# Expert stage of a transformer block: gathers in halves behind the products, both experts take rows back, other weight pages held for the accumulators

## The chip, the cores and the metric

One core of a Trainium2 chip runs the kernel. Its engines are TensorE (PE in the profile), VectorE (DVE), ScalarE (ACT), GpSimd (POOL) and SyncE (SP), which here issues nearly all DMA transfers. The metric is the device time of one execution in microseconds (us); lower is better.

## The reference

One block over 512 latent tokens of width 1024 (with 256 context tokens): modulation, two attentions in parallel, a layer norm, then a mixture of 16 experts in which each expert picks its 64 tokens, and a second layer norm. The change lies in the mixture:

```python
def ec_moe(h, w_router, b_router, w1, w3, w2):
    b, n, _ = h.shape
    cap = EC_CAPACITY * n // N_EXPERTS              # 64
    aff = jax.nn.softmax((h @ w_router + b_router).astype(jnp.float32), axis=-1)
    g, idx = lax.top_k(jnp.swapaxes(aff, 1, 2), cap)
    bidx = jnp.arange(b)[:, None, None]
    xe = h[bidx, idx]
    hid = jax.nn.silu(jnp.einsum('becd,edf->becf', xe, w1)) * jnp.einsum('becd,edf->becf', xe, w3)
    ye = jnp.einsum('becf,efd->becd', hid, w2) * g[..., None].astype(h.dtype)
    return jnp.zeros_like(h).at[bidx, idx].add(ye)

x = layer_norm(ALPHA * x + g1 * o_lat, ln1_g, ln1_b)
x = layer_norm(ALPHA * x + g2 * ec_moe(x * (1.0 + sc2) + sh2, *moe), ln2_g, ln2_b)
```

All is float32. w1, w3 and w2 are 1024 x 1024 for each expert, 201 MB in all.

## The kernel before, in words

The expert stage is the last part of the kernel, from about 557 us on. It works through eight pairs of experts. A weight matrix comes in 8 pieces of 128 x 1024 (512 KB each), by `load` (line 940), so a pair takes 48 pieces: 32 of w1 and w3 (the up products), 16 of w2 (the down products).

**Pages.** `order` is the list of the pieces in the order of their use. Pieces go into a ring of 36 SBUF pages (`prefetch`); a page is used again when TensorE has read the piece in it. SyncE issues the loads one after the other, so a load whose page is still in use holds back all behind it. Nine more pieces are loaded ahead, once, into the places of tiles that are needed only later (`hold`, `places`): the four accumulators `acc0` to `acc3`, the tiles `gb`, `ye`, `hid`, `ohT` and `hidT`. The key in `places` is the position in `order`: 0 to 15 are w1 and w3 of expert 0 in turn, 16 to 31 those of expert 1, 32 to 39 w2 of expert 0, 40 to 47 w2 of expert 1. A held piece gives its place to the tile when it has been read, but frees no page of the ring. So 45 pieces are loaded before the first product ends.

**One pair.** `gather` makes a one-hot matrix `oh` on VectorE (L1133) and lets TensorE pick the pair's 128 token rows, transposed, out of `xn` (L1143): eight steps ("eighths") of 4 matmuls; after four and after eight of them VectorE writes `xe` (L1148). `up_` multiplies with w1 and w3 (L1180): eight steps k of two pieces; ScalarE and VectorE make `hid` (L1182, L1183). `back` scales `oh` on GpSimd (L1155) and transposes it (L1160) for putting rows back. `hid_t` transposes `hid` (L1188). `down` multiplies with w2 (L1196). `scatter` scales and splits the result on VectorE and ScalarE and gives four steps of two matmuls (L1209), each added to an accumulator on VectorE (L1210), for one half of the columns. The rows of a pair are put back during the next pair (`waiting`).

**Order.** TensorE's order is that of the code; the other engines' is a scheduler's. `base`, called once after the first pair's up products, loads ln1's scale and shift by GpSimd's queue and writes the first value of the accumulators: GpSimd the left half of the columns, VectorE the right (L1222, L1223). It ends with `spread` (L118), two matmuls that broadcast g2 into `g2b`.

Of the kernel before, what the change touches and what calls it, by code (L numbers as in the profile page):

```python
# [10 lines left out]
F32 = mybir.dt.float32  # L11
# [13 lines left out]
KD = D // 128  # L25
# [27 lines left out]
def _layer(tc, A, out, opened):  # L53
# [62 lines left out]
    def spread(dst, i, p, ps):  # L116

        T.matmul(ps, one2[p:p + 1, 0:1].to_broadcast([1, 128]), rm[i][p:p + 1, :], start=True, stop=True)  # L118
        S.activation(dst, ps, AF.Copy)
# [691 lines left out]
    for h in range(HEADS):  # L811
        pr = h // 2
# [86 lines left out]
    for c in range(4):  # L899
        hl = wos[c]  # L900
        for jj in range(2):
# [3 lines left out]
            g = yt.tile([128, 512], F32, name="gy")  # L905
# [19 lines left out]
    order[-2 * KD:] = [(E_N - 2 + i, "w2", (q, kh)) for q, p in enumerate(PARTS) for kh in range(KD // p[2]) for i in range(2)]  # L925
    loaded = {}

    places = {2: "gb", 5: "ye", 8: "acc0", 10: "acc1", 12: "acc2", 13: "hid", 16: "acc3", 21: "ohT", 27: "hidT"}
    order_r = [i for i in range(len(order)) if i not in places]
    N_RING = N_PG + N_WS + N_PG2 + N_PG3  # L930
    ring = [0]
# [1 line left out]
    def load(i, t):  # L933
        e, nm, k = order[i]
        if isinstance(k, tuple):
            q, kh = k
            c0, w, ks = PARTS[q]
            dma(t[:, :ks * w].rearrange("p (k n) -> p k n", k=ks), wsrc[nm][e, :, ks * kh:ks * kh + ks, c0:c0 + w])
        else:
            dma(t, wsrc[nm][e, :, k, :])  # L940
        loaded[e, nm, k] = t

    def place(nm):
        return rM if nm in ("gb", "acc0") else rM2 if nm[:3] == "acc" else me

    def hold(nm):
        load(next(i for i in places if places[i] == nm), place(nm).tile([128, D], F32, name="wr", tag=nm, bufs=1))
# [166 lines left out]
    psd, _ = pool("psd", space=PSUM)  # L1114
# [3 lines left out]
        return rM2.tile(shape or [128, D], dt, name=name, tag="pg3", bufs=N_PG3)  # L1118


    for nm in ("acc1", "acc2", "acc3"):
        hold(nm)
    prefetch(N_PG3)
    for nm in ("ye", "hid", "ohT", "hidT"):
        hold(nm)
    acc = [place(f"acc{t}").tile([128, D], F32, name="acc", tag=f"acc{t}", bufs=1) for t in range(NT)]

    def gather(pr):
# [23 lines left out]
    def back(pr, o):  # L1152

        e0 = 2 * pr
        G.tensor_tensor(o, o, aff[:, :, e0:e0 + 2, None].to_broadcast([128, NT, 2, CAP]), op=OP.mult)  # L1155
        ohT = me.tile([128, 2, SEQ], F32R, name="ohT")
        gt = me.tile([128, 2], F32, name="gate", bufs=2)
        ps = psd.tile([128, 512], F32, name="mx", bufs=3)
        for t in range(NT):
            T.transpose(ps[:, t * 128:(t + 1) * 128], o[:, t].rearrange("p e s -> p (e s)"), ident)  # L1160
        S.activation(ps, ps, AF.Copy, accum_out=gt[:, 0:1])
        V.tensor_scalar(ohT[:, 0, :], ps, 0.0, None, op0=OP.is_gt)
        if pr + 1 < E_N // 2:
            for e in range(2):
                a, b = slice(64 * e, 64 * e + 64), slice(64 - 64 * e, 128 - 64 * e)
                S.activation(ohT[b, 1, :], f(ohT[a, 0, :]), AF.Copy)
                S.activation(gt[b, 1:2], gt[a, 0:1], AF.Copy)
        return ohT, gt

    def up_(e, xe, hid, between=None, at=KD // 2):  # L1170

        sl = slice((e % 2) * CAP, (e % 2) * CAP + CAP)
        ph = [psd.tile([128, 512], F32, name="h", bufs=3) for _ in range(2)]
        for k in range(KD):
            if k == at and between:
                between()
            for i, n in enumerate(("w1", "w3")):
                w = piece(e, n, k)
                for hf in range(2):
                    T.matmul(ph[i][64 * hf:64 * hf + 64, :], xe[:, k, sl], w[:, hf * 512:(hf + 1) * 512],  # L1180
                             start=k == 0, stop=k == KD - 1)
        S.activation(hid[:, e % 2, :], ph[0], AF.Silu)  # L1182
        V.tensor_tensor(hid[:, e % 2, :], hid[:, e % 2, :], ph[1], op=OP.mult)  # L1183
# [15 lines left out]
    def scatter(py, ohT, gt, hf):  # L1199

        hs = slice(hf * 512, (hf + 1) * 512)
        ye = me.tile([128, 2, 512], F32R, name="ye")
        V.scalar_tensor_tensor(py[hf], py[hf], gt[:, hf:hf + 1], g2b[:, hs], op0=OP.mult, op1=OP.mult)  # L1203
        split(ye[:, 0, :], ye[:, 1, :], py[hf])

        def tile_(t):
            ps = psd.tile([128, 512], F32, name="mx", bufs=3)
            for i in range(2):
                T.matmul(ps, ohT[:, hf, t * 128:(t + 1) * 128], ye[:, i, :], start=i == 0, stop=i == 1)  # L1209
            V.tensor_tensor(acc[t][:, hs], acc[t][:, hs], ps, op=OP.add)  # L1210
        return [lambda t=t: tile_(t) for t in range(NT)]

    def base():

        gb = [me.tile([128, 2, 512], F32, name="gb0", tag="ye", bufs=1), rM.tile([128, 2, 512], F32, name="gb1", tag="gb", bufs=1)]
        for hf in range(2):
            for i, nm in enumerate(("ln1_g", "ln1_b")):
                G.dma_start(gb[hf][:, i], A[nm][:, hf * 512:(hf + 1) * 512].to_broadcast([128, 512]))
        for hf, eng in enumerate((G, V)):
            hs = slice(hf * 512, (hf + 1) * 512)  # L1220
            for t in range(NT):
                eng.tensor_tensor(acc[t][:, hs], xn[t][:, hs], gb[hf][:, 0], op=OP.mult)  # L1222
                eng.tensor_tensor(acc[t][:, hs], acc[t][:, hs], gb[hf][:, 1], op=OP.add)  # L1223
        g2b = rM.tile([128, D], F32, name="g2b", tag="gb", bufs=1)
        for g in range(2):
            spread(g2b[:, g * 512:(g + 1) * 512], 1, 64 + 32 * g, psd.tile([128, 512], F32, name="mx", bufs=3))
        return g2b

    def run(steps):
        for fn in steps:  # L1230
            fn()
# [3 lines left out]
    xe, o, steps = gather(0)  # L1235
    run(steps[:4])
    waiting = None
    for pr in range(E_N // 2):
        last = pr == E_N // 2 - 1
        hid = me.tile([128, 2, 512], F32, name="hid")  # L1240
        if waiting:
            s0 = scatter(*waiting, 0)
            up_(2 * pr, xe, hid, lambda: run(s0))
            run(scatter(*waiting, 1))
            ohT, gt = back(pr, o)
        else:
            up_(2 * pr, xe, hid, lambda: run(steps[4:]), 2)
        up_(2 * pr + 1, xe, hid)
        if not waiting:
            ohT, gt = back(pr, o)  # L1250
        hT = me.tile([128, 2, 4, 2, CAP], F32, name="hidT")
        hid_t(hid, hT, 0)
        if last:
            hid_t(hid, hT, 1)
            break
        xe, o, steps = gather(pr + 1)
        run(steps)
        hid_t(hid, hT, 1)
        if pr == 0:
            g2b = base()  # L1260
        py = [psd.tile([128, 512], F32, name="y", bufs=2) for _ in range(2)]
        for i in range(2):
            down(2 * pr + i, hT, py)
        waiting = py, ohT, gt
# [11 lines left out]
    ye = me.tile([128, 2, 512], F32R, name="ye")  # L1276
# [59 lines left out]
    for t in range(NT):  # L1336
        o = acc[t]
# [53 lines left out]
```

## Time and profile before

| what | value |
|---|---|
| median of 3 runs | 1047.92 us (1045.59 to 1049.13) |
| the profiled execution | 1046.86 us |
| its span, first to last instruction | 1045.0 us |
| PE, DVE, ACT, POOL busy | 94%, 43%, 26%, 17% of the span |
| loads of expert weights | 388, mostly 512 KB |

The profile is of one execution. The span is 1.86 us shorter than the execution's time. A busy PE is not a PE at its peak, and PE's instructions include ones that stretch while they wait for data. In the profile every matmul of the program in float32 is two instructions (the order below counts the program's).

### The profile page before, as it was taken

The numbers are of one execution on the slowest core, as the hardware profiler recorded it, in microseconds if no ns is written. First come the engines' busy times: TensorE is split into PE (matmuls) and PEld (weight loads), VectorE is DVE, ScalarE is ACT, GpSimd is POOL, SyncE is SP. The second block draws the span as 40 slices with busy tenths as digits, with TensorE's granted clock in tenths as the row PEclk, the third lists the DMA queues.
The fourth block names the chain that finished last, engine by engine and source line by source line (L and its number), as shares of the span: only waits on it lengthen the run. The fifth ranks groups of instructions, "written<-read, shape, count | busy, mean of one in ns | idle before, by whom it ended". The sixth has DMA issues, their size and how long they took to land.

```text
span 1045.0 us, 13829 instructions
## 1 busy us (share of the span) xinstructions
PE 981.9 (94%) x5280; PEld 618.1 (59%) x5280; DVE 445.7 (43%) x871; ACT 276.9 (26%) x556; POOL 173.7 (17%) x176
## 2 busy tenths in 40 slices
PE   6999998989899999999997999999999999999982
PEld 5888976868787777777754443535353534234331
DVE  2382366762677556558473413122213131111236
ACT  1222324224777555544110101010101010010010
POOL 2340020202576422210021400000000000000004
PEclk9999998999999999999998999999999999999996
DMA  9944337762012000038947989999999999999992
GB/s 298 291 155 131 98 113 250 233 200 82 21 31 66 22 20 22 21 107 305 393 177 308 377 307 409 409 409 409 408 409 409 410 409 409 409 410 409 408 367 100
DMA packets 101210, 266.98 MB, mean 255 GB/s; under 512 B 14020, under 2 KB 37528, under 8 KB 101144
## 3 DMA queue, kind: packets, MB, share of 16 engines
q1 hardware_dynamic: 100248, 264.52, 68.2%
q0 software_dynamic: 320, 1.05, 0.3%
q8 instruction: 42, 0.69, 0.3%
q10 hardware_dynamic: 576, 0.52, 0.1%
q14 instruction: 24, 0.20, 0.1%
HBM read 261.47 MB, written 2.10 MB: 252 GB/s over the span
## 4 chain that ended last, share of the span: by engine, by line
PE 71%; DMA 10%; issue 9%; DVE 5%; POOL 2%; ACT 2%; SPq 0%; POOLq 0%; DVEq 0%; ACTq 0%
PE h L1180 15%; PE y L1196 8%; DMA wr<-moe_w 6%; PE mx L1143 6%; PE acc L84 5%; PE acc L83 5%; PE acc L82 5%; PE sc L653 5%; DMA wa<-w_ada 3%; PE tpb L661 3%; PE av L843 2%; PE mx L1209 2%; PE av L778 2%; PE tp L237 1%; PE po L84 1%
## 5 line engine op out<-in xcount | busy, mean ns | idle before, releaser
L1180 PE MATMUL h<-wr,xe 128*64 128x512 f32 x1024 | 233.7, 598 | 8.6 <-DMA wr<-moe_w 7.5
L1180 PEld LDWEIGHTS h<-wr,xe 128*64 128x64 f32 x1024 | 68.3, 136 | 162.8 <-issue 105.7
L1196 PE MATMUL y<-wr,hidT 128*64 128x512 f32 x448 | 97.7, 594 | 0.0
L1183 DVE TENSOR_TENSOR hid<-hid,h 128x512 f32<-128x512 f32 x16 | 11.0, 686 | 146.8 <-PE h L1180 146.8
L642 DVE TENSOR_REDUCE nm<-sc 128x1 f32<-128x768 f32 x64 | 60.2, 954 | 30.7 <-PE sc L653 29.5
L1196 PEld LDWEIGHTS y<-wr,hidT 128*64 128x64 f32 x448 | 31.5, 137 | 61.8 <-issue 57.6
L1155 POOL TENSOR_TENSOR oh<-oh,aff 128x512 f32<-128x512 f32 x8 | 8.4, 1047 | 351.0 <-PE mx L1143 351.0
L643 ACT ACTIVATE P<-sc,nm 128x768 f32<-128x768 f32 x64 | 57.5, 900 | 29.0 <-DVE nm L642 21.8
L1143 PE MATMUL mx<-oh,xn 128*128 128x128 f32 x512 | 61.1, 282 | 1.4 <-DVE oh L1133 1.4
L1143 PEld LDWEIGHTS mx<-oh,xn 128*128 128x128 f32 x512 | 60.1, 198 | 2.5 <-issue 1.3
L75 ACT ACTIVATE whi<-wraw 128x1024 fp32r<-128x1024 f32 (+1 forms) x32 | 33.5, 1047 | 97.7 <-DMA wraw<-w_in 63.3
L78 DVE TENSOR_TENSOR wlo<-wraw,whi 128x1024 fp32r<-128x1024 f32 (+1 forms) x32 | 39.0, 1219 | 45.2 <-PE acc L83 29.4
L75 ACT ACTIVATE ye<-y 128x512 fp32r<-128x512 f32 (+2 forms) x17 | 9.7, 572 | 180.2 <-DVE y L1203 98.7
L1210 DVE TENSOR_TENSOR acc<-acc,mx 128x512 f32<-128x512 f32 x56 | 34.6, 680 | 42.0 <-PE mx L1209 42.0
L82 PE MATMUL acc<-xlh,whi 128*128 128x512 f32 x128 | 50.9, 398 | 1.6 <-ACT whi L75 1.6
L1182 ACT ACTIVATE hid<-h 128x512 f32<-128x512 f32 x16 | 9.6, 597 | 154.9 <-PE h L1180 154.9
L82 PE MATMUL acc<-whi,xlh 128*128 128x512 f32 (+1 forms) x128 | 49.6, 391 | 1.0 <-ACT whi L75 1.0
L84 PE MATMUL acc<-xlh,wlo 128*128 128x512 f32 x128 | 49.5, 394 | 0.8 <-DVE wlo L78 0.8
L83 PE MATMUL acc<-xll,whi 128*128 128x512 f32 x128 | 50.1, 391 | 0.0
L1203 DVE SCALAR_TENSOR_TENSOR y<-y,gate,g2b 128x512 f32<-128x512 f32 x14 | 9.9, 754 | 92.6 <-PE y L1196 92.6
L84 PE MATMUL acc<-whi,xll 128*128 128x512 f32 (+1 forms) x128 | 48.7, 381 | 0.5 <-POOL xll L78 0.5
L83 PE MATMUL acc<-wlo,xlh 128*128 128x512 f32 (+1 forms) x128 | 48.8, 381 | 0.2 <-DVE wlo L78 0.2
(341 smaller groups left out, 1699.3 us busy)
## 6 DMA issues: line engine op xcount, KB each, us to landing
wr<-moe_w SPq DMA_DIRECT2D x372, 512.0 KB, 10.2
wa<-w_ada SPq DMA_DIRECT2D x32, 512.0 KB, 4.4
wraw<-w_in SPq DMA_DIRECT2D x28, 512.0 KB, 5.1
wa<-w_ada SPq DMA_DIRECT2D x8, 1024.0 KB, 9.7
wr<-moe_w SPq DMA_DIRECT2D x16, 384.0 KB, 8.4
outraw<-w_out SPq DMA_DIRECT2D x8, 512.0 KB, 9.8
xq<-x SPq DMA_DIRECT2D x4, 512.0 KB, 7.9
q<-q SPq DMA_DIRECT2D x16, 128.0 KB, 2.2
```

The source lines that it names most:

```text
L75: S.activation(hi, src, AF.Copy)
L78: (eng_lo or V).tensor_tensor(lo, src, f(hi), op=OP.subtract)
L82: T.matmul(ps, lh, rh, start=start, stop=False)
L83: T.matmul(ps, lh, rl, start=False, stop=False)
L84: T.matmul(ps, ll, rh, start=False, stop=stop)
L642: V.tensor_reduce(nm, ps[:, :768], axis=AX.X, op=OP.max, negate=True)
L643: S.activation(p, ps[:, :768], AF.Exp, bias=nm, accum_out=z)
L653: T.matmul(ps[:, a:b], l, r[:, a:b], start=i == 0, stop=i == len(passes) - 1)
L1143: T.matmul(pss[hf][:, kk * 128:(kk + 1) * 128], xn[t][:, k * 128:(k + 1) * 128], o[:, t].rearrange("p e s -> p (e s)"), start=t == 0, stop ...
L1180: T.matmul(ph[i][64 * hf:64 * hf + 64, :], xe[:, k, sl], w[:, hf * 512:(hf + 1) * 512], start=k == 0, stop=k == KD - 1)
L1196: T.matmul(py[hf][r0:r0 + 64, :], hT[:, e % 2, fc % 4, fc // 4, :], w[:, hf * 512:(hf + 1) * 512], start=fc == 0, stop=fc == KD - 1)
L1210: V.tensor_tensor(acc[t][:, hs], acc[t][:, hs], ps, op=OP.add)
```

## The change

Three things change in the expert stage.

1. `places`: the four accumulators now hold w2 pieces (32 to 35) in place of early up pieces; `hid`, `ohT` and `hidT` hold up pieces 14, 29 and 30. All held pieces but two are loaded ahead of the last three pages of the ring.
2. From the second pair on, only the first four eighths of a gather stand between up and down products; the last four run inside the next pair's first expert, ahead of k = 3. The rows of the pair before are put back at k = 6 of the first expert (it was k = 4) and at k = 3 of the second expert (it was between the experts). `back` comes after both experts in every pair.
3. `base` no longer runs `spread`; its two matmuls run inside the second pair, behind the four eighths ahead of k = 3. Its loads come in the other order.

```diff
-    places = {2: "gb", 5: "ye", 8: "acc0", 10: "acc1", 12: "acc2", 13: "hid", 16: "acc3", 21: "ohT", 27: "hidT"}
+    places = {2: "gb", 5: "ye", 14: "hid", 29: "ohT", 30: "hidT", 32: "acc0", 33: "acc1", 34: "acc2", 35: "acc3"}
...
-    for nm in ("acc1", "acc2", "acc3"):
+    for nm in ("ye", "hid", "ohT", "hidT", "acc1", "acc2", "acc3"):
         hold(nm)
     prefetch(N_PG3)
-    for nm in ("ye", "hid", "ohT", "hidT"):
-        hold(nm)
...
-    def up_(e, xe, hid, between=None, at=KD // 2):
+    def up_(e, xe, hid, between={}):
...
         for k in range(KD):
-            if k == at and between:
-                between()
+            if k in between:
+                run(between[k])
...
-        for hf in range(2):
+        for hf in (1, 0):
             for i, nm in enumerate(("ln1_g", "ln1_b")):
...
         g2b = rM.tile([128, D], F32, name="g2b", tag="gb", bufs=1)
-        for g in range(2):
-            spread(g2b[:, g * 512:(g + 1) * 512], 1, 64 + 32 * g, psd.tile([128, 512], F32, name="mx", bufs=3))
-        return g2b
+        return g2b, [lambda g=g: spread(g2b[:, g * 512:(g + 1) * 512], 1, 64 + 32 * g, psd.tile([128, 512], F32, name="mx", bufs=3))
+                     for g in range(2)]
...
         if waiting:
-            s0 = scatter(*waiting, 0)
-            up_(2 * pr, xe, hid, lambda: run(s0))
-            run(scatter(*waiting, 1))
-            ohT, gt = back(pr, o)
+            rows_ = []
+            up_(2 * pr, xe, hid, {3: steps[4:] + spread_, 4: [lambda: rows_.extend(scatter(*waiting, 0))],
+                                  6: [lambda: run(rows_)]})
+            spread_ = []
+            rows_ = scatter(*waiting, 1)
+            up_(2 * pr + 1, xe, hid, {3: rows_})
         else:
-            up_(2 * pr, xe, hid, lambda: run(steps[4:]), 2)
-        up_(2 * pr + 1, xe, hid)
-        if not waiting:
-            ohT, gt = back(pr, o)
+            up_(2 * pr, xe, hid, {2: steps[4:]})
+            up_(2 * pr + 1, xe, hid)
+        ohT, gt = back(pr, o)
...
         xe, o, steps = gather(pr + 1)
-        run(steps)
+        run(steps[:4])
         hid_t(hid, hT, 1)
         if pr == 0:
-            g2b = base()
+            g2b, spread_ = base()
```

On TensorE, from the end of the first pair's up products (L1180 x56) to the middle of the second pair, the program before has these rows; the rows left out repeat the gather's matmul (L1143), 32 in all between the transposes.

```order
L1180 MATMUL h<-wr,xe 64x512 x56
L1160 MATMUL mx<-ident,oh 128x128 x4
L1188 MATMUL mx<-ident,hid 128x128 x4
L1143 MATMUL mx<-oh,xn_4497 128x128
...
L1188 MATMUL mx<-ident,hid 128x128 x4
L118 MATMUL mx<-rm,one_65 128x512 x2
L1196 MATMUL y<-wr,hidT 64x512 x32
L1180 MATMUL h<-wr,xe 64x512 x16
L1209 MATMUL mx<-ye,ohT 128x512 x8
```

The same place in the changed program, where L1141 is the gather (16 rows at each of its two places here), L1178 the up product, L1194 the down product and L1207 the rows put back.

```order
L1178 MATMUL h<-wr,xe 64x512 x56
L1158 MATMUL mx<-ident,oh 128x128 x4
L1186 MATMUL mx<-ident,hid 128x128 x4
L1141 MATMUL mx<-oh,xn_4497 128x128
...
L1186 MATMUL mx<-ident,hid 128x128 x4
L1194 MATMUL y<-wr,hidT 64x512 x32
L1178 MATMUL h<-wr,xe 64x512 x12
L1141 MATMUL mx<-oh,xn_4497 128x128
...
L118 MATMUL mx<-rm,one_65 128x512 x2
L1178 MATMUL h<-wr,xe 64x512 x12
L1207 MATMUL mx<-ye,ohT 128x512 x8
```

Sixteen gather matmuls and the two of `spread` have moved from ahead of the down products to behind the first three steps of the next up products, and the rows put back come at the seventh step, not the fifth.

On SyncE, these are the loads into the accumulators' places (the first three), the last pages and the other held tiles of the program before, with the first two loads into used pages behind them (the number is that of the tile, the right name the weight matrix).

```order
L940 DMA wr_5142<-moe_w1 128x1024
L940 DMA wr_5144<-moe_w1 128x1024
L940 DMA wr_5146<-moe_w1 128x1024
L940 DMA wr_5148<-moe_w2 128x1024
L940 DMA wr_5150<-moe_w2 128x1024
L940 DMA wr_5152<-moe_w2 128x1024
L940 DMA wr_5154<-moe_w3 128x1024
L940 DMA wr_5156<-moe_w3 128x1024
L940 DMA wr_5158<-moe_w3 128x1024
L940 DMA wr_5160<-moe_w3 128x1024
L940 DMA wr_5417<-moe_w2 128x1024
L940 DMA wr_5421<-moe_w2 128x1024
```

The same place in the changed program.

```order
L940 DMA wr_5150<-moe_w2 128x1024
L940 DMA wr_5152<-moe_w2 128x1024
L940 DMA wr_5154<-moe_w2 128x1024
L940 DMA wr_5156<-moe_w2 128x1024
L940 DMA wr_5142<-moe_w3 128x1024
L940 DMA wr_5144<-moe_w1 128x1024
L940 DMA wr_5146<-moe_w3 128x1024
L940 DMA wr_5148<-moe_w1 128x1024
L940 DMA wr_5158<-moe_w2 128x1024
L940 DMA wr_5160<-moe_w2 128x1024
L940 DMA wr_5390<-moe_w2 128x1024
L940 DMA wr_5394<-moe_w2 128x1024
```

The accumulators' places now get w2, the four tiles `ye`, `hid`, `ohT` and `hidT` get their pieces two loads earlier, and the up pieces that those places no longer hold lie in pages of the ring.

## Rows read from the trace of the kernel before

**Rows 1.** The page: engines, then DMA share (tenths) and GB/s in 40 slices.

```profile
PE 981.9 (94%) x5280; PEld 618.1 (59%) x5280; DVE 445.7 (43%) x871; ACT 276.9 (26%) x556; POOL 173.7 (17%) x176
...
DMA  9944337762012000038947989999999999999992
```

**Rows 2.** Windows: length; busy by engine (PE, PEld, DVE, ACT, POOL); PEclk, DMA share, GB/s.

```profile
557.00:562.00 5.00, 5.00 (x27) 5.00 (x27) 0.00 (x0) 1.22 (x1) 0.00 (x0) 0.57 0.97 385
562.00:572.00 10.00, 9.42 (x62) 5.73 (x61) 2.60 (x8) 0.06 (x1) 2.36 (x3) 1.00 0.58 211
572.00:578.00 6.00, 6.00 (x30) 2.00 (x28) 2.54 (x5) 0.00 (x0) 1.13 (x2) 1.00 0.80 220
578.00:582.00 4.00, 4.00 (x22) 1.42 (x20) 3.40 (x3) 0.60 (x1) 3.52 (x3) 1.00 1.03 415
582.00:588.00 6.00, 6.00 (x32) 2.00 (x30) 3.01 (x3) 0.00 (x0) 5.84 (x5) 1.00 0.99 350
588.00:602.00 14.00, 13.83 (x94) 8.78 (x91) 3.33 (x8) 3.43 (x8) 2.08 (x2) 1.00 1.03 413
602.00:608.00 6.00, 6.00 (x34) 3.18 (x34) 1.37 (x4) 1.79 (x3) 1.05 (x1) 1.00 0.12 41
608.00:613.00 5.00, 5.00 (x26) 1.62 (x24) 0.00 (x0) 0.00 (x0) 0.00 (x0) 1.00 0.96 310
613.00:623.00 10.00, 10.00 (x50) 3.39 (x48) 2.11 (x3) 0.60 (x1) 0.00 (x0) 1.00 1.03 413
683.00:853.00 170.00, 170.00 (x880) 75.81 (x881) 41.20 (x79) 18.67 (x37) 3.14 (x3) 1.00 1.03 409
853.00:983.00 130.00, 123.76 (x602) 49.29 (x600) 29.85 (x56) 13.43 (x27) 2.10 (x2) 1.00 1.03 409
```

**Rows 3.** SyncE's waits from 594 to 607: us, times, longest.

```profile
SPq L940 <- PE y L1196: 11.5, 1, 11.5
SPq L940 <- PE h L1180: 0.9, 2, 0.5
```

**Rows 4.** Timeline of SyncE from 606: start us, us, loads.

```profile
606.81 14.31 SPq L940 DMA_DIRECT2D wr<-moe_w  x16
```

**Rows 5.** Chain that ended last, 594 to 680: start us, us, what.

```profile
593.63 1.31 PE h L1180 x6
...
595.64 0.43 DVE oh L1133
...
596.11 7.41 PE mx L1143 x64
603.52 0.44 PE mx L1188 x4
603.96 1.81 PE mx L118 x4
605.77 13.88 PE y L1196 x64
619.65 6.87 PE h L1180 x32
626.52 2.18 PE mx L1209 x8
...
660.54 13.88 PE y L1196 x64
674.42 5.58 PE h L1180 x26
```

**Rows 6.** Timeline of TensorE, last pair and tail: start us, us, idle before.

```profile
958.70 3.71 PE L1180 MATMUL h<-wr,xe 128*64 128x512 f32 x16
...
998.22 0.66 PE L1188 MATMUL mx<-ident,hid 128*128 128x128 f32 x4
...
1007.67 1.50 PE L1317 MATMUL y<-wr,hidT 128*64 128x384 f32 x6 [0.19 <-DMA wr<-moe_w]
```

**Rows 7.** Lines from 556 to 700: busy us, mean ns.

```profile
L1148 DVE TENSOR_SCALAR xe<-mx,ghv,bhv 128x128 f32<-128x128 f32 x24 | 8.2, 403 | 23.3 <-PE mx L1143 23.3
L1222 POOL TENSOR_TENSOR acc<-xn,gb 128x512 f32<-128x512 f32 x4 | 6.0, 1500 | 4.2 <-PE h L1180 4.2
L1160 PE MATMUL mx<-ident,oh 128*128 128x128 f32 x12 | 1.9, 282 | 0.0
```

**Rows 8.** Timeline of VectorE, `base` beside GpSimd's half from 578.2 on.

```profile
577.66 0.69 DVE L1223 TENSOR_TENSOR acc<-acc,gb 128x512 f32<-128x512 f32 x1
...
580.08 1.65 DVE L1223 TENSOR_TENSOR acc<-acc,gb 128x512 f32<-128x512 f32 x1
```

**Rows 9.** SyncE's wait for the router's threshold, 553 to 556.

```profile
SPq L940 <- DVE top L1085: 3.3, 1, 3.3
```

**Rows 10.** TensorE's waits from 556 to 853: us, times, longest.

```profile
PE mx L1143 <- DVE oh L1133: 1.4, 2, 1.2
PE h L1180 <- DVE xe L1148: 0.6, 1, 0.6
```

## The prediction

> **What bounds the kernel now.** I read the page first. TensorE is busy for 94% of the span, but the DMA row stands at its top for the last 16 slices [rows 1]. The windows say what that means: from 613 on the core moves 409 to 413 GB/s without a break, to 983, whatever TensorE does [rows 2]. A piece of 512 KB (0.524 MB) takes 0.524/409 = 1.28 us, a pair's 48 pieces 61.4 us. TensorE needs less: from one start of down products to the next it goes 605.77 to 660.54 [rows 5], 54.8 us. So in every pair the loads fall 6.6 us behind TensorE, and TensorE runs out of its lead: from 853 on it is idle in places [rows 2], and the last pair's up products start at 958.70 [rows 6], where five pairs of 54.8 us from 674.42 [rows 5] would be at 948.3. The end is therefore set by when the last load lands, and that by how long the transfers stood still before 613, since later there is nothing to win back.
>
> The same windows show the stops. From 562 to 572 half the rate is lost: all 45 places are full and the first product has hardly freed a page. From 572 to 578 it is 220 GB/s, from 582 to 588 350. Then comes the large one: 41 GB/s from 602 to 608, 310 from 608 to 613 [rows 2]. SyncE's waits name the cause: one wait of 11.5 us for a down product [rows 3], ended at 606.81, after which 16 loads go out in 14.3 us [rows 4]. The chain shows what TensorE did meanwhile: up products to 594.9, then gather 7.41, transposes 0.44, spread 1.81, and only then the first down product, at 605.77 [rows 5]. None of this reads weights, so no page comes free for 11 us.
>
> **The change, part by part.**
>
> *Held pieces.* Of the 32 up pieces nine were held before, so 23 freed a ring page by 595. Now five are (positions 2, 5, 14, 29, 30), so 27 do. Before, the 23 loads took the transfers to 602.6 (602 plus 41 GB/s x 6 us = 0.25 MB, 0.6 us). Four more take 5.1 us: to 607.7. The price: w2's first four pieces of expert 0 now sit in the accumulators, so the first page that a down product frees is that of the fifth. A down piece takes 13.88/16 = 0.87 us [rows 5].
>
> *Gather in halves, spread moved.* Between up and down products now stand half a gather (7.41/2 = 3.7) and the transposes (0.44). Down starts at 596.11 + 3.7 + 0.44 = 600.25 instead of 605.77. The fifth piece is read at 600.25 + 4.35 = 604.6, and its load goes out 0.2 later (before: first piece read at 606.64, load at 606.81), at 604.8. Data of a restarted queue flows about 1.1 us after the issue (41 GB/s until 608, issue 606.81), thus at 605.9, before the queue runs dry at 607.7. Pages then come every 0.87 us against 1.28 for a load. The stop closes. What it cost: 11 us at 409 GB/s are 4.50 MB, moved were 41 x 6 + 310 x 5 = 1.80 MB; the missing 2.70 MB are **6.6 us**. The handover is thin (1.8 us of margin); its cost lies between 0 and the 1.2 us that 608 to 613 lost after the restart, and since the queue shouldn't empty, I take 0.3.
>
> The Trainium skill ("DMA: Bandwidth & Descriptors", Specifications) gives one core some 358 GB/s of HBM. The trace doesn't agree, it shows 409 to 413. By the page's rate the missing 2.70 MB would be 7.5 us and the sum -6.9; the measured rate stands.
>
> *The earlier stretches.* 562 to 572 stays: the pieces read first are placed as before up to position 6. In 572 to 588 pages come earlier (no held piece among positions 6 to 13, before four). But 578 to 582 ran at 415 GB/s with the old pages, so pages weren't the limit there, and ln1's broadcast loads lie in 572 to 578 in both. The bounds are 0 and a gain of 0.9 (582 to 588 at full rate) plus some 1.0 of the 2.8 before; I take 0.
>
> *What the moved work does in the second pair.* Down ends at 614.1, three steps k end at 619.3, then half a gather and spread, 5.5 us, hold the pages again: the next comes at 625.7. By 619.3 the loads for 45 freed pages are due (27 + 12 + 6), and by 625.7 the transfers have done 23 + (625.7 - 602.6)/1.28 = 41. Four pieces are left, 5 us of work; 1.1 us go for the restart, so about 3.8 us of margin. At the next gap (rows put back, 2.2 us, page at 633.1) it is 51 less 47, the same. Later the margin grows by 6.6 us a pair.
>
> *Rows put back later, back later.* These are the same instructions at other places, each under products. The half gather's `xe` (4 x 0.40 on VectorE [rows 7]) has one step, 1.74 us, of products as cover; where there is none, at the first gather, TensorE waited 0.6 [rows 10]. The one-hot matrix of the next pair is now made after the products (0.43 [rows 5]), some 0.2 of it bare, as in the first pair today (1.4 in two waits, of which the first gather's is 1.2 [rows 10]). TensorE can bear this: its second pair of down products ends about 671.0 (674.4 before), five pairs of 54.8 make 944.9, and the loads let the last pair begin at 958.7 - 6.3 = 952.4. That is 7.5 us, 1.5 a pair, and 5 more in the last pair's up products (32 loads of 1.28 = 41.0 against 27.8 of products, 3.7 of gather and 4.4 of rows put back). In the tail `back`'s transposes (12 for three pairs in 1.9, so 0.6 [rows 7]) now stand between the last up products and the final ones, at 998.22; TensorE has caught up with the loads by 1007.67 with 0.19 to spare [rows 6]. Bounds 0 and 0.6; I take 0.3.
>
> *Loads ahead of the wait.* SyncE waits 3.3 us for the router's threshold [rows 9]. Two more loads are now behind it. I cost it at nothing: the rate to 562 was 385 GB/s [rows 2], so loads lay queued across the wait, and half of 562 to 572 stands empty anyway. Without that cover it is at most two pieces, 2.6 us.
>
> *`base`.* It can write an accumulator only when its piece has been read in the down products, from 601.1 on. Sixteen instructions: VectorE's take 0.69 alone and up to 1.65 beside GpSimd [rows 8], GpSimd's 1.50 [rows 7]. In parallel, or one after another at 0.69, they are done by 618.6 (8 x 0.69 + 8 x 1.50 = 17.5); VectorE's next piece of work for TensorE is the second half of `xe` at 623.
>
> **Sum.** -6.6 + 0.3 + 0 + 0.3 = -6.0 from the profiled execution's 1046.86: 1040.9. The median of the runs lies 1.06 higher; I go a little toward it and name **1041.2**. About 0.3% (3.1 us) is what a measurement of this kernel can tell from no change.
>
> **The rivals.**
>
> *A, the stop only shrinks.* If TensorE comes to the down products late by d, transfers stop for d - 1.8 and lose 1.2 more. With the start unmoved (605.77; d = 5.5) the fifth piece's load goes at 610.3: a stop of 3.7 + 1.2, and 6.6 - 4.9 = 1.7 is left: 1045.2; a smaller d lies between. For it: four products free no page. Against: the rows moved out of the gap are seen in TensorE's order.
>
> *B, `base` blocks the second pair.* If VectorE's eight all take 1.65 and none overlaps with GpSimd, 8 x 1.65 + 8 x 1.50 = 25.2 us end at 626.3; `xe` follows at 627.9, and TensorE, which would want it at 626.6, waits 1.3 us. Within the 3.8 us of margin this costs nothing: 1041. It decides from 5 us on. The Trainium skill ("SBUF — State Buffer", section "SBUF: two separate sides") states the rule behind it: VectorE with two SBUF inputs and GpSimd take turns on a shared port pair, the loser blocked for a whole instruction. The trace agrees as far as it goes, with 0.69 become 1.65.
>
> *C, TensorE becomes the bound (slower).* The place is step 4 of every pair: products wait for `xe` behind whatever VectorE has queued (two scalings, a split, the additions). At 4 us a pair, six pairs give 24, less 12.6 of slack: 11.4 us late, 1052.3. It takes over from 2.1 us a pair and makes the kernel 0.3% slower from 3.7 (12.6 + 6.3 + 3.1 over six). Against: the widest wait of this kind is 0.6, and `xe` has cover.
>
> *D, no change.* The gap closes, but the lost time comes back elsewhere, such as a stop in the second pair above 3.8 us of lateness. 1045 to 1048.
>
> **How the numbers follow.** Forecast (1038.5 to 1042.5, B within it) 0.74; A 0.13; D 0.05; C 0.08. A's part under 1044.8 goes to faster: faster 0.79, same 0.13, slower 0.08. The low end takes the bounds of the early stretches: 1040.9 - 1.9 - 0.6 = 1038.4. The high end takes A in, 1045.2, and some of the spread of the runs: 1046.0. Left out are C, part of D, and little below.
>
> **What would show it.** Right: no slice between 588 and 983 below 400 GB/s; SyncE's longest wait for a down product 2 us or less; down products starting near 600.3; all of the later stages earlier by 6 us with the last transfers. Wrong: a window near 605 or 625 with a low rate; TensorE waiting for VectorE at step 4 or 6; transfers running on while the span doesn't shrink, which would move the bound to TensorE.

## The result and the profile after

| what | before | after |
|---|---|---|
| median, runs taken side by side | 1048.12 us (6 runs, 1045.02 to 1049.54) | 1040.94 us (6 runs, 1039.21 to 1042.25) |
| ratio after/before, 95% interval | | 0.9938 [0.9921, 0.9954] |
| the profiled execution, its span | 1046.86 us, 1045.0 us | 1040.02 us, 1038.2 us |

The change makes the kernel 0.6% faster. The windows of the changed kernel, over the stretches of [rows 2] (length; PE, PEld, DVE, ACT, POOL busy; PEclk, DMA share, GB/s):

```profile
562.00:572.00 10.00, 9.43 (x65) 6.22 (x65) 1.97 (x6) 0.00 (x0) 1.86 (x3) 1.00 0.63 227
572.00:578.00 6.00, 6.00 (x30) 2.00 (x28) 0.77 (x3) 0.00 (x0) 1.63 (x3) 1.00 0.65 195
578.00:582.00 4.00, 4.00 (x20) 1.29 (x18) 0.08 (x1) 0.60 (x1) 0.00 (x0) 1.00 1.01 367
582.00:588.00 6.00, 6.00 (x30) 2.00 (x28) 0.60 (x1) 0.00 (x0) 0.00 (x0) 1.00 1.03 419
588.00:602.00 14.00, 13.83 (x86) 7.66 (x84) 3.33 (x8) 4.03 (x9) 0.00 (x0) 1.00 1.02 408
602.00:608.00 6.00, 6.00 (x32) 2.00 (x28) 5.90 (x5) 0.00 (x0) 5.72 (x4) 1.00 1.03 408
608.00:613.00 5.00, 5.00 (x26) 1.59 (x24) 4.97 (x4) 0.00 (x0) 4.92 (x4) 1.00 0.99 380
613.00:623.00 10.00, 10.00 (x61) 5.18 (x58) 1.51 (x1) 0.00 (x0) 2.56 (x2) 1.00 1.03 412
...
853.00:983.00 130.00, 126.99 (x628) 52.97 (x628) 31.92 (x60) 13.03 (x26) 2.10 (x2) 1.00 1.03 409
```

The large stop is gone: 408 and 380 GB/s where 41 and 310 stood. In bytes (rate times length), 602 to 613 moved 4.35 MB and not 1.80: 2.55 MB, 6.2 us at 409 GB/s. Over 562 to 588 it is 7.42 instead of 7.19 MB (0.6 us gained), in the other windows to 623 0.08 MB less (0.2 us lost). Together 2.70 MB, 6.6 us. The same stretch in finer slices, the DMA view of 600 to 625 in 40 slices of 0.625 us, first before, then after:

```profile
GB/s 406 400 406 288 92 20 0 0 0 26 0 0 98 334 419 308 275 197 308 334 354 406 387 413 406 419 420 419 426 413 433 400 413 406 400 419 420 413 400 419
```

```profile
GB/s 406 419 413 406 400 406 413 406 413 406 413 393 413 387 380 321 354 406 354 406 400 419 406 426 419 419 419 400 406 419 413 400 419 419 406 413 413 400 400 413
```

Before, the rate falls to nothing from the fourth slice (602) on and is not whole again until the 22nd (613). After, only a dent is left, down to 321 GB/s at 609. The chain that ended last, from the same place as [rows 5], shows what TensorE does in the meantime:

```profile
596.74 3.84 PE mx L1141 x32
600.58 0.44 PE mx L1186 x4
601.01 13.88 PE y L1194 x64
614.90 5.15 PE h L1178 x24
620.05 3.77 PE mx L1141 x32
623.82 1.06 PE mx L118 x4
```

The down products begin at 601.01 instead of 605.77. The other half of the gather and `spread` stand at 620.05 to 624.88, and the transfers go through them at 412 and 409 GB/s. The last pair begins 7.2 us earlier than in [rows 6], and still waits for data there (timeline of TensorE):

```profile
951.47 2.27 PE L1178 MATMUL h<-wr,xe 128*64 128x512 f32 x8 [0.29 <-DMA wr<-moe_w]
```

### The profile page after: what moved, and what is told of

It reads as the page before. It is cut to its first block, busy times and chain, and to the rows that moved or that the text cites. A ratio compares the mean times of both kernels' runs of the same rounds, so it can differ in the third digit from the quotient of the medians.

```text
span 1038.2 us, 13837 instructions
## 1 busy us (share of the span) xinstructions
PE 978.0 (94%) x5280; PEld 619.0 (60%) x5280; DVE 451.0 (43%) x871; ACT 276.2 (27%) x556; POOL 175.8 (17%) x176
## 4 chain that ended last, share of the span: by engine, by line
PE 76%; DMA 8%; issue 7%; DVE 5%; POOL 2%; ACT 2%; POOLq 0%; SPq 0%; DVEq 0%; ACTq 0%
PE h L1178 17%; PE y L1194 8%; PE acc L84 6%; PE acc L83 6%; PE acc L82 6%; PE mx L1141 6%; DMA wr<-moe_w 5%; PE sc L653 5%; PE tpb L661 3%; PE av L843 2%; PE mx L1207 2%; PE av L778 2%; PE tp L237 2%; DMA wa<-w_ada 1%; PE po L84 1%
## 5 line engine op out<-in xcount | busy, mean ns | idle before, releaser
L1178 PE MATMUL h<-wr,xe 128*64 128x512 f32 x1024 | 229.5, 596 | 3.6 <-DMA wr<-moe_w 2.7
L1178 PEld LDWEIGHTS h<-wr,xe 128*64 128x64 f32 x1024 | 69.9, 137 | 148.8 <-issue 113.5
L1194 PE MATMUL y<-wr,hidT 128*64 128x512 f32 x448 | 98.3, 594 | 0.5 <-DMA wr<-moe_w 0.4
L1194 PEld LDWEIGHTS y<-wr,hidT 128*64 128x64 f32 x448 | 31.3, 137 | 62.6 <-issue 56.1
L1141 PEld LDWEIGHTS mx<-oh,xn 128*128 128x128 f32 x512 | 60.5, 197 | 10.7 <-issue 7.0
L1141 PE MATMUL mx<-oh,xn 128*128 128x128 f32 x512 | 63.5, 284 | 2.4 <-DVE oh L1131 2.4
L1208 DVE TENSOR_TENSOR acc<-acc,mx 128x512 f32<-128x512 f32 x56 | 34.7, 681 | 66.5 <-PE mx L1207 66.5
L1146 DVE TENSOR_SCALAR xe<-mx,ghv,bhv 128x128 f32<-128x128 f32 x64 | 21.8, 403 | 85.7 <-PE mx L1141 85.7
L1180 ACT ACTIVATE hid<-h 128x512 f32<-128x512 f32 x16 | 9.6, 597 | 160.5 <-PE h L1178 160.5
```

The lines of the kernel that those rows point to most:

```text
L1141: T.matmul(pss[hf][:, kk * 128:(kk + 1) * 128], xn[t][:, k * 128:(k + 1) * 128], o[:, t].rearrange("p e s -> p (e s)"), start=t == 0, stop ...
L1194: T.matmul(py[hf][r0:r0 + 64, :], hT[:, e % 2, fc % 4, fc // 4, :], w[:, hf * 512:(hf + 1) * 512], start=fc == 0, stop=fc == KD - 1)
```

## The experiments

Twelve runs follow, of ten further kernels, one of them twice, and of the changed kernel once more. They ran in four comparisons, each beside the kernel before (its medians 1047.56, 1047.58, 1047.70 and 1048.26 us). One measure recurs, here called the **lag**: the time from the first up product until only 160 MB are left to move of all that SyncE's queue moves (summed over the transfers of the trace; nearly all of it loads). The smaller, the earlier the last load lands. It is needed since the expert stage does not begin at the same time in every execution, and since single medians scatter by 1 to 2 us. Before, 160 MB are left at 629.5 and the first up product begins at 563.3, a lag of 66.2 us; after, 623.4 and 563.9, a lag of 59.5 us. When the first up product begins, the same 180.4 MB are left in both.

### Which part closed the stop

*Places alone*: the new `places` and order of the held loads, with TensorE's order of before (the diff is against the kernel before; all others are against the changed kernel).

```diff
-    places = {2: "gb", 5: "ye", 8: "acc0", 10: "acc1", 12: "acc2", 13: "hid", 16: "acc3", 21: "ohT", 27: "hidT"}
+    places = {2: "gb", 5: "ye", 14: "hid", 29: "ohT", 30: "hidT", 32: "acc0", 33: "acc1", 34: "acc2", 35: "acc3"}
...
-    for nm in ("acc1", "acc2", "acc3"):
+    for nm in ("ye", "hid", "ohT", "hidT", "acc1", "acc2", "acc3"):
         hold(nm)
     prefetch(N_PG3)
-    for nm in ("ye", "hid", "ohT", "hidT"):
-        hold(nm)
```

> The new held pieces and their load order alone; TensorE's order is that of before. Theory of the prediction (the stop at 602 is closed by TensorE coming earlier to the down products, the held pages add four loads): down products still start near 605.8, the fifth piece is read at 610.1, its load goes out at 610.3, while four loads more carry the transfers to 607.7; the stop shrinks from 5.4 us to about 3.7 and the time falls by 2 us (1 to 3). Rival (the held pages do it): the time falls by 5 us or more. Rival (the pages moved to w2 cost what they give): within 1 us of before.

Measured: 1044.9 us, ratio 0.9974 [0.9961, 0.9987]. Its windows and the chain:

```profile
602.00:608.00 6.00, 6.00 (x49) 5.37 (x48) 2.71 (x8) 0.60 (x1) 1.04 (x1) 1.00 1.03 409
608.00:613.00 5.00, 5.00 (x23) 1.51 (x23) 3.07 (x4) 0.00 (x0) 2.96 (x2) 1.00 0.43 168
613.00:623.00 10.00, 10.00 (x49) 3.31 (x46) 9.32 (x6) 0.56 (x2) 9.76 (x7) 1.00 0.86 313
```

```profile
608.86 6.15 PE y L1194 x27
```

The stage began at 566.4 in this execution, 3.1 us later than before, and the down products 3.1 us later too: TensorE's order is that of before. The four added loads hold until 608, then the stop comes, shorter. This is what the prediction's rival A describes. It was given 1.7 us; the medians show 2.7 (1.4 to 4.1 over the interval), and the lag, 64.2 us (160 MB left at 630.6), is 2.0 less than before.

*Order alone*: the changed kernel with the old places (and the old order of the held loads).

```diff
-    places = {2: "gb", 5: "ye", 14: "hid", 29: "ohT", 30: "hidT", 32: "acc0", 33: "acc1", 34: "acc2", 35: "acc3"}
+    places = {2: "gb", 5: "ye", 8: "acc0", 10: "acc1", 12: "acc2", 13: "hid", 16: "acc3", 21: "ohT", 27: "hidT"}
...
-    for nm in ("ye", "hid", "ohT", "hidT", "acc1", "acc2", "acc3"):
+    for nm in ("acc1", "acc2", "acc3"):
         hold(nm)
     prefetch(N_PG3)
+    for nm in ("ye", "hid", "ohT", "hidT"):
+        hold(nm)
```

> The new order on TensorE (half gathers, spread inside the second pair, rows put back later, back behind both experts) with the held pieces of before. Theory: down products start near 600.5 and free a page with the first piece, at 601.3, so data flows again at 602.5, just when the 23 loads run dry (602.6): the stop closes almost as well as in the full change, 5.5 us less than before (4 to 6.5). The two parts then overlap: their gains alone add up to more than the whole. Rival (the held pages do it): 2 us or less gained.

Measured: 1040.81 us, ratio 0.9937 [0.9924, 0.9950].

```profile
602.00:608.00 6.00, 6.00 (x30) 2.01 (x28) 0.00 (x0) 0.00 (x0) 0.00 (x0) 1.00 1.00 345
608.00:613.00 5.00, 5.00 (x26) 1.60 (x24) 0.00 (x0) 0.00 (x0) 0.00 (x0) 1.00 1.02 411
```

The order gives the time of the whole change: 6.7 us, a little more than expected. The old places free fewer pages by the end of the up products, but the first down piece frees one at once; the new ones free four more, and the first down piece that frees one is the fifth. Once the gap is short, either leaves only a small stop: 345 and 411 GB/s here against 408 and 380. In lag the places are still worth something: 160 MB are left at 623.4, the first up product is at 562.2, and the lag of 61.2 us is 1.7 us more than with both. The medians, 0.1 us apart and from different comparisons, do not show it.

*`spread` back in the gap*, all else changed: `base` calls `spread` again, ahead of the down products.

```diff
-        return g2b, [lambda g=g: spread(g2b[:, g * 512:(g + 1) * 512], 1, 64 + 32 * g, psd.tile([128, 512], F32, name="mx", bufs=3))
-                     for g in range(2)]
+        for g in range(2):
+            spread(g2b[:, g * 512:(g + 1) * 512], 1, 64 + 32 * g, psd.tile([128, 512], F32, name="mx", bufs=3))
+        return g2b, []
```

> The full change, but the two spread matmuls (1.1 to 1.8 us) stand ahead of the first pair's down products again. Theory: the fifth piece is read about 1.5 us later, its load goes out near 606.8 and data flows near 607.9, against a queue that in the changed kernel holds at least 2 us of work at that point: 0 to 0.8 us slower than the changed kernel. Rival (every us that TensorE is late at this place is lost, there is no margin): 1.1 to 1.8 us slower.

Measured: 1041.89 us, ratio 0.9948 [0.9932, 0.9964]. Its windows:

```profile
602.00:608.00 6.00, 6.00 (x27) 2.21 (x27) 3.95 (x7) 0.60 (x1) 2.49 (x2) 1.00 1.03 410
608.00:613.00 5.00, 5.00 (x26) 1.69 (x24) 5.00 (x4) 0.00 (x0) 4.92 (x4) 1.00 0.89 306
613.00:623.00 10.00, 10.00 (x50) 3.19 (x46) 6.89 (x6) 1.68 (x3) 5.80 (x4) 1.00 1.00 390
```

The down products begin 1.8 us later against the first up product, and the lag is 60.9 us, 1.4 more than with the whole change. Of the delay of 1.8 us, 0.4 was taken up and 1.4 lost, where 0 to 0.8 were expected. The medians differ by 0.95 us, inside the intervals: the loss is read from one trace, not from the times.

*Rows put back where they were*, at k = 4 of the first expert and between the experts, with `back` there.

```diff
-            rows_ = []
-            up_(2 * pr, xe, hid, {3: steps[4:] + spread_, 4: [lambda: rows_.extend(scatter(*waiting, 0))],
-                                  6: [lambda: run(rows_)]})
+            s0 = []
+            up_(2 * pr, xe, hid, {3: steps[4:] + spread_ + [lambda: s0.extend(scatter(*waiting, 0))],
+                                  4: [lambda: run(s0)]})
             spread_ = []
-            rows_ = scatter(*waiting, 1)
-            up_(2 * pr + 1, xe, hid, {3: rows_})
+            run(scatter(*waiting, 1))
+            ohT, gt = back(pr, o)
+            up_(2 * pr + 1, xe, hid)
...
-        ohT, gt = back(pr, o)
+            ohT, gt = back(pr, o)
```

> The full change, but the rows of the pair before are put back at k = 4 of the first expert and between the experts, and back stands between the experts, as before the change. Theory: these places are covered by loads, the same time as the changed kernel within 0.7 us; in the second pair TensorE waits some 2 to 3 us at k = 4 for g2b and the scaled rows, inside the margin of 3.8 us. Rival (the later places of the rows are a part of the gain): 1.5 us or more slower than the changed kernel.

Measured: 1041.37 us, ratio 0.9942 [0.9929, 0.9955], lag 59.3 us. In TensorE's waits from 556 to 853 two new ones appear, of the rows put back:

```profile
PE mx L1207 <- ACT ye L75: 0.3, 1, 0.3
PE mx L1207 <- DVE ye L78: 0.2, 1, 0.2
```

They are 0.5 us, once, where 2 to 3 us were expected, and the lag does not change. The later places of the rows, and of `back`, are worth nothing that can be measured.

### What sets the end

*Six loads less*: in six pairs the last piece of the even expert's w1 is not loaded and the piece before it is used in its place. TensorE's work stays the same; the output does not. The diff leaves out the lines that use the piece before it.

```diff
+    order = [x for x in order if not (x[1] == "w1" and x[2] == KD - 1 and x[0] in range(2, 14, 2))]
...
```

> The full change with six loads of 512 KB left out, one for each of the pairs two to seven (the last w1 piece of the pair's first expert is not loaded; its products read the piece before it, so the output differs). TensorE's work is the same. Theory (the loads set the end): 6 x 1.28 = 7.7 us faster than the changed kernel. Rival (TensorE sets the end): no faster, at most 1 us.

Measured: 1032.91 us, ratio 0.9864 [0.9836, 0.9893]. The changed kernel's 0.9938 less this is 0.0074, of 1048 us 7.8 us, with intervals that leave this uncertain by some 3 us. The window before the last pair:

```profile
853.00:983.00 130.00, 129.66 (x654) 56.71 (x652) 32.47 (x60) 13.02 (x26) 2.10 (x2) 1.00 1.03 409
```

*Half of the work on rows put back*: the two matmuls that add up to a step of L1207 become one, so the output differs.

```diff
-            for i in range(2):
-                T.matmul(ps, ohT[:, hf, t * 128:(t + 1) * 128], ye[:, i, :], start=i == 0, stop=i == 1)
+            for i in range(1):
+                T.matmul(ps, ohT[:, hf, t * 128:(t + 1) * 128], ye[:, i, :], start=True, stop=True)
```

> The full change with half of the matmuls that put rows back left out (the low half of the split, L1207, in all but the last pair, so the output differs in its low digits): some 1.1 us less for each half, 2.2 us less TensorE work a pair, 15 us in all; the loads are the same. Theory (the loads set the end): within 0.7 us of the changed kernel. Rival (TensorE sets the end): 8 us faster or more.

Measured: 1039.47 us, ratio 0.9932 [0.9905, 0.9958].

```profile
853.00:983.00 130.00, 122.92 (x594) 47.27 (x592) 29.39 (x55) 12.42 (x25) 2.10 (x2) 1.00 1.03 409
```

In the same window TensorE is busy for 4.1 us less than after, and the rate is the same 409 GB/s. Taking work from TensorE lets it idle more and shortens nothing that can be measured (1.5 us in the medians, more than the 0.7 expected but inside the intervals; the rival's 8 is outside); taking 3.1 MB from the loads gives 7.8 us, where 3.1/0.409 are 7.7. With these six loads gone TensorE is idle for 0.34 of 130 us, so it is then all but the bound itself.

*The gather's half without cover*, at k = 4, where its `xe` is needed at once:

```diff
-            up_(2 * pr, xe, hid, {3: steps[4:] + spread_, 4: [lambda: rows_.extend(scatter(*waiting, 0))],
+            up_(2 * pr, xe, hid, {4: steps[4:] + spread_ + [lambda: rows_.extend(scatter(*waiting, 0))],
```

> The full change, but the second half of a gather (and in the second pair spread) stands ahead of k = 4, not k = 3: the products behind it need the xe that it has just made, so nothing covers VectorE's work on it. Theory (loads are the bound, TensorE has 7 to 12 us to give by the last pair): TensorE waits some 0.6 us in each of the pairs two to eight, 4 us in all, and the time is that of the changed kernel within 0.7 us. Rival C of the prediction in small (TensorE's waits reach the end): 2 to 4 us slower than the changed kernel.

Measured: 1040.54 us, ratio 0.9938 [0.9919, 0.9957]. TensorE's waits from 556 to 853, first of the changed kernel, then that for `xe` of this one:

```profile
PE mx L1141 <- DVE oh L1131: 2.0, 6, 1.2
PE h L1178 <- DVE xe L1146: 0.6, 1, 0.6
```

```profile
PE h L1178 <- DVE xe L1146: 2.1, 4, 0.6
```

Three waits of 0.5 us for `xe` are new, one in each pair from the third on; in the second pair `spread` stands between and covers it. The time does not move: TensorE has that to spare.

### Whether more can be had

*Early pages*: `gb` and `ye` hold pieces 7 and 9, not 2 and 5, and the first gather's second half runs ahead of k = 3, not 2.

```diff
-    places = {2: "gb", 5: "ye", 14: "hid", 29: "ohT", 30: "hidT", 32: "acc0", 33: "acc1", 34: "acc2", 35: "acc3"}
+    places = {7: "gb", 9: "ye", 14: "hid", 29: "ohT", 30: "hidT", 32: "acc0", 33: "acc1", 34: "acc2", 35: "acc3"}
...
-            up_(2 * pr, xe, hid, {2: steps[4:]})
+            up_(2 * pr, xe, hid, {3: steps[4:]})
```

> The full change, and in the first pair more pages free early: gb and ye hold pieces 7 and 9 in place of 2 and 5, and the first gather's second half stands at k = 3, not k = 2. This goes for the stop from 562 to 578, which the prediction left as it was. Theory (a page freed early is a load that starts early while the queue is empty): two more loads ahead of the gather's second half, 1 to 2.5 us faster than the changed kernel. Rival (ln1's broadcast loads, now later, take from the queue what they did not take before): within 0.7 us of the changed kernel.

Measured: 1041.33 us, ratio 0.9945 [0.9924, 0.9966].

```profile
562.00:572.00 10.00, 9.74 (x60) 5.62 (x62) 1.73 (x6) 0.00 (x0) 0.51 (x1) 1.00 0.76 282
572.00:578.00 6.00, 6.00 (x30) 2.01 (x28) 0.80 (x3) 0.00 (x0) 2.94 (x5) 1.00 0.78 229
...
602.00:608.00 6.00, 6.00 (x32) 2.00 (x30) 6.00 (x5) 0.00 (x0) 5.84 (x5) 1.00 0.99 373
608.00:613.00 5.00, 5.00 (x26) 1.62 (x24) 4.80 (x3) 0.00 (x0) 4.84 (x4) 1.00 0.98 377
```

Against the first up product, the queue comes down to 170 MB after 34.1 us, where the changed kernel needs 34.7: 0.6 us are won, not the 1 to 2.5 expected. But from 602 to 613 less is moved (4.12 MB, 4.35 after): transfers that run ahead use up the freed pages sooner and then wait for the fifth down piece (SyncE's longest wait for a down product is 5.1 us here, 4.1 after). The lag is 59.4 us, as after. What little is won early is lost again at the handover.

*Accumulators later*: they hold w2's pieces 36 to 39, so that the first down piece frees a page.

```diff
-    places = {2: "gb", 5: "ye", 14: "hid", 29: "ohT", 30: "hidT", 32: "acc0", 33: "acc1", 34: "acc2", 35: "acc3"}
+    places = {2: "gb", 5: "ye", 14: "hid", 29: "ohT", 30: "hidT", 36: "acc0", 37: "acc1", 38: "acc2", 39: "acc3"}
```

> The accumulators hold pieces 36 to 39 (the second four of w2 of expert 0) in place of 32 to 35, all else as in the changed kernel. Theory (the handover hangs on the first down product that frees a page): the first down piece now frees a page at once, 4 x 0.87 = 3.5 us earlier, so nothing is lost at the handover: 608 to 613 moves 400 GB/s or more (380 in the changed kernel) and SyncE's longest wait for a down product ends 3.5 us earlier. Worth 0.0 to 0.4 us, so the same time, 1040.5 to 1041. base starts 3.5 us later and ends near 619, still ahead of the xe at 623. Rival (base is the next bound): TensorE waits for VectorE at the second pair's fourth step, 1 us or more, and the rate falls below 400 GB/s in 623 to 633.

Measured: 1040.85 us, ratio 0.9927 [0.9903, 0.9951].

```profile
608.00:613.00 5.00, 5.00 (x26) 1.69 (x24) 4.79 (x4) 0.00 (x0) 4.69 (x3) 1.00 1.02 408
```

The lag is 59.1 us, 0.4 less. No dent shows here, but that is no proof: in its second profile (below) the changed kernel itself has none,

```profile
608.00:613.00 5.00, 5.00 (x26) 1.61 (x24) 4.96 (x4) 0.00 (x0) 4.92 (x4) 1.00 1.03 405
```

with a lag of 59.4. What the accumulators' later pieces are worth is not shown. `base` ran later, beside 608 to 623, and the time stayed the same.

*All held pieces later*: these accumulators, and `gb`, `hid`, `ye` at 13, 14, 15, with the first gather's second half ahead of k = 3. It ran twice, the second time beside the changed kernel itself.

```diff
-    places = {2: "gb", 5: "ye", 14: "hid", 29: "ohT", 30: "hidT", 32: "acc0", 33: "acc1", 34: "acc2", 35: "acc3"}
+    places = {13: "gb", 14: "hid", 15: "ye", 29: "ohT", 30: "hidT", 36: "acc0", 37: "acc1", 38: "acc2", 39: "acc3"}
...
-            up_(2 * pr, xe, hid, {2: steps[4:]})
+            up_(2 * pr, xe, hid, {3: steps[4:]})
```

> As the kernel with the accumulators at 36 to 39, and gb, hid and ye hold pieces 13, 14 and 15, so that the first 13 pieces read all free a page of the ring; the first gather's second half runs ahead of k = 3. Theory (in 562 to 582 the loads wait for pages that products free): the rate of 562 to 582 rises from 227, 195 and 367 GB/s by more than in the version with gb and ye at 7 and 9 (282, 229, 355), and what is won there, 0.6 to 2 us, isn't lost at the handover this time, because the first down piece frees a page at once: the last 160 MB begin 0.6 to 2 us earlier against the first product than in the changed kernel, and the time is 1039 to 1040.5. Rival (the early stretch is bound by TensorE's own start, or by the 45 places): no more than 0.5 us of lead against the first product, time as the changed kernel's.

> The changed kernel once more, to stand on the same chip beside the version with all held pieces later (accumulators at 36 to 39, gb, hid and ye at 13 to 15). Both theories: 1040.5 to 1041.5, as in its own runs.

> The version with all held pieces later once more, beside the changed kernel on the same chip. In its first profile the last 160 MB began 1.75 us earlier against the first product than in the changed kernel's, while the medians differed by 2.6 us. Theory (a lead won early and kept through the handover shortens the end one for one): 1.5 to 2.5 us below the changed kernel in this same comparison, and the same lead against the first product in the second profile, 1.5 to 2 us. Rival (the first difference was the scatter of runs of 2 us, and the early lead is lost later): within 1 us of the changed kernel.

First comparison: 1038.26 us, ratio 0.9916 [0.9895, 0.9937]. Second: 1039.70 us, 0.9916 [0.9892, 0.9940], beside the changed kernel's 1039.68 us, 0.9916 [0.9893, 0.9940], which was expected at 1040.5 to 1041.5. The second profile's windows:

```profile
572.00:578.00 6.00, 6.00 (x31) 2.22 (x31) 1.36 (x4) 0.00 (x0) 1.05 (x1) 1.00 0.92 312
...
608.00:613.00 5.00, 5.00 (x26) 1.72 (x24) 5.00 (x4) 0.00 (x0) 4.92 (x4) 1.00 1.03 409
```

The lag is smaller in both, 57.7 and 57.8 us, against 59.5 and 59.4 in the changed kernel's two profiles, and nothing is lost at the handover. In the first comparison, without the changed kernel beside it, that went with a lower median; in the second, with it, not, as the rival had it. In the second profile the 1.6 us are lost to the clock in the tail (timeline of TensorE, the last 32 products, first of the changed kernel in that comparison, then of this one; under it the latter's window):

```profile
1013.76 3.67 PE L1315 MATMUL y<-wr,hidT 128*64 128x256 f32 x32
```

```profile
1011.95 5.31 PE L1315 MATMUL y<-wr,hidT 128*64 128x256 f32 x32
```

```profile
1013.00:1016.00 3.00, 3.00 (x20) 1.71 (x18) 1.60 (x7) 0.00 (x0) 0.00 (x0) 0.61 0.02 10
```

These products start 1.81 us earlier and end 0.17 us earlier: for part of the time the granted clock was at the lower of its two levels, 1.2 GHz (mean 0.61 in the window). That is one execution and does not account for the medians. Whether this version is faster than the changed kernel is therefore not settled: loads ahead by 1.6 us are shown, a shorter time than the changed kernel's is not. Both beat the kernel before.

## Why the prediction was right

**What bounds the end** (loads 6.6 us a pair slower than TensorE): shown. Six loads less gave what six loads take, and half of the work on rows taken from TensorE gave nothing beyond the interval.

**The stop of 6.6 us closes:** right. 2.70 MB more are moved by 623, 2.55 of them in the stop itself. The lag, which counts from the first product, is 6.7 us less. The down products start at 601.01, 0.8 us later than forecast: this execution's stage began 0.6 us later, and the half gather takes 3.84 and not 3.7.

**The handover:** the cost was right; the margin of 1.8 us is not shown. The dent of 380 GB/s in 608 to 613 is 0.15 MB or 0.4 us (0.3 forecast); in the second profile, at 405 GB/s, it is under 0.1. But `spread` put back, which delays the down products by just these 1.8 us, costs 1.4. Either the margin was only 0.4, or it was there and the restart then took its 1.2; this run doesn't tell the two apart. Rival A's rule, which uses both (late by d, d less 1.8 plus 1.2 are lost), holds in size: 1.2 where 1.4 is measured, and 4.8 for the places alone (d is 5.4), where the lag is 4.7 more than with both.

**Held pieces:** the four added loads do lengthen the transfers to 608, as places alone shows. But the prediction used both parts as if both were needed. By its own numbers the places win 5.1 us and give up 4 x 0.87 = 3.5, so 1.6 net; the lag shows 1.7 on top of the order and 2.0 without it, and the order alone reaches the same median.

**Earlier stretches:** counted at 0, with a gain of up to 1.9; they gave 0.6 by the windows to 588, and 0.5 and 0.3 in the two profiles if the bytes are counted 38 us after the first up product (168.85 MB left before, 168.63 and 168.73). The reason given for 0, that pages were not the limit, holds for 578 to 582 alone: the version with `gb`, `hid` and `ye` at 13 to 15 moved 312 to 364 GB/s from 572 to 578 in its two profiles, where the changed kernel moved 195 and 231 in its own.

**Second pair and TensorE:** 412 and 409 GB/s through the second gap, and rows put back at their old place cost nothing. Rival C is out: no wait for `xe` at step k = 4, and 0.5 us a pair without cover. The one-hot waits are 2.0 us in six, where 0.2 a pair on top of the first 1.2 were forecast.

**Loads ahead of the wait:** counted at nothing, rightly. SyncE's wait for the router's threshold is longer in this execution (548 to 564),

```profile
SPq L940 <- DVE top L1085: 6.0, 1, 6.0
```

but the 180.4 MB left at the first up product are those of before.

**`base`:** hidden, rival B as well. Both engines run it side by side (timelines of VectorE and GpSimd):

```profile
602.07 0.69 DVE L1220 TENSOR_TENSOR acc<-xn,gb 128x512 f32<-128x512 f32 x1
602.80 1.64 DVE L1221 TENSOR_TENSOR acc<-acc,gb 128x512 f32<-128x512 f32 x1
```

```profile
614.04 1.60 POOL L1221 TENSOR_TENSOR acc<-acc,gb 128x512 f32<-128x512 f32 x1
```

Beside GpSimd's, VectorE's take 1.64 to 1.76 as rival B had it, but the records of the two overlap and can't be added up: all 16 are done in 13.6 us, at 615.64, 8 us ahead of `xe` at 623.86.

**Signs that were wrong:** no slice was to fall below 400 GB/s; the dent did, and cost 0.4 us. And the text asked for a longest wait of SyncE of 2 us or less. From 594 to 607 it is

```profile
SPq L940 <- PE y L1194: 4.6, 2, 4.1
```

and yet the transfers run: issued loads were still under way. How long the issuer waits says little by itself; whether the transfers stop is what counts.

**The sum:** -6.0 forecast, the two profiled executions differ by 6.84, the ratio by 6.5 of 1048 us (4.8 to 8.3 over its interval). Of the 6.84, 1.5 belong to the clock in the tail of the execution of before (below), which leaves 5.4. The last products that wait for data come 5.4 us earlier too, against [rows 6]:

```profile
1002.31 1.50 PE L1315 MATMUL y<-wr,hidT 128*64 128x384 f32 x6 [0.16 <-DMA wr<-moe_w]
```

The point of 160 MB came 6.1 us earlier (629.5, 623.4: the lag's 6.7 less the 0.6 by which the stage began later). Why 0.7 us less arrive at the last products stays open. `back`'s 0.3 in the tail may be a part, but the kernel with `back` at its old place was no faster (1041.37 us). That -6.0 lies within 1 us of all three measures (5.4, 6.5, 6.84) is in part luck: its terms for the handover and the tail are smaller than what one execution differs from the next.

## What to carry to other kernels

Where a ring of buffers feeds an engine, look for the stretches in which the engine works on things that free no buffer, and split or move that work until the issued transfers outlast each stretch; here 5.4 us less of such work (half a gather, 3.6, and `spread`, 1.8) were enough for the whole gain. Count the buffers freed up to the end of a stretch and the time of the first one freed behind it as one sum, since a change that adds to the one may take from the other. Time saved ahead of the next such stretch is kept only if that one has room for it.

## What the runs showed of the hardware

**The granted clock in the tail.** The last 32 products took 3.67 us in six of the fourteen profiles and 4.5 to 5.3 in the other eight, though they are the same products. Before:

```profile
1018.51 1.48 PE L1297 MATMUL mx<-ye,ohT 128*128 128x384 f32 x4 [0.30 <-DVE acc L1301]
1019.92 4.75 PE L1317 MATMUL y<-wr,hidT 128*64 128x256 f32 x32
```

```profile
1016.00:1019.00 3.00, 1.73 (x6) 1.02 (x7) 1.85 (x5) 0.49 (x1) 0.00 (x0) 0.95 0.95 346
1019.00:1022.00 3.00, 3.00 (x14) 1.73 (x14) 3.00 (x14) 0.00 (x0) 0.00 (x0) 0.50 0.42 162
```

and after, with the clock whole:

```profile
1013.10 1.08 PE L1295 MATMUL mx<-ye,ohT 128*128 128x384 f32 x4 [0.30 <-DVE acc L1299]
1014.11 3.67 PE L1315 MATMUL y<-wr,hidT 128*64 128x256 f32 x32
```

Before, the clock fell to the lower level (0.50, 1.2 GHz) late in a stretch in which TensorE was busy for 1.73 of 3 us, and the 32 products took 1.08 us more, the four matmuls ahead of them 0.40 more. After an idler stretch of the changed kernel, 1.34 of 3 us,

```profile
1010.00:1013.00 3.00, 1.34 (x6) 0.66 (x4) 1.69 (x4) 0.49 (x1) 0.00 (x0) 1.00 1.06 374
```

it did not fall. So one such stretch does not decide it, and what does stays open. The 32 products alone vary by up to 1.6 us in this way (5.31 against 3.67), also between two executions of one kernel (all held pieces later: 3.67, then 5.31), which is as much as the smaller experiments were to tell apart.

**The start of the stage**, taken as that of the first up product, lay between 562.2 and 566.9 us over all profiles (563.1 and 563.9 in the two of the changed kernel itself). The start of a later piece of work in one trace can't be set against that in another; its distance from an event of the same execution can.
